# Spreading the sums of the output weights and the latent heads' parts over other heads of a hybrid attention block

## The chip, the cores and the metric

The kernel runs on one core of a Trainium2 chip. The metric is the device time of one execution in microseconds (us); three executions of the kernel before are given. Five engines work beside each other: TensorE (PE, the matmuls), VectorE (DVE), ScalarE (ACT), GpSimd (POOL, here mostly the issuer of small transfers) and SyncE (SP, the issuer of the weight loads).

## The reference, cut to what matters

```python
def hybrid_layer(x, cos, sin, pre_norm_w, w_in, ..., w_out, post_norm_w):     # x: 1 x 512 x 2048, float32
    h = rms_norm(x, pre_norm_w)
    sb_q, sb_k, sb_v, sb_gate, c_q, c_kv, k_rope, mla_gate = jnp.split(h @ w_in, split_pts, axis=-1)
    o_a = stick_breaking_attention(sb_q, sb_k, sb_v)          # 8 heads of 128, strictly causal
    ...
    o_b = chunk_causal_softmax_attention(q_mla, k_mla, v_mla)     # 8 heads from low-rank latents
    mixed = jnp.concatenate([o_a * jax.nn.silu(sb_gate), o_b * jax.nn.silu(mla_gate)], axis=-1)
    y = mixed @ w_out                                         # 512 x 2048 by 2048 x 2048
    return x + rms_norm(y, post_norm_w)
```

In stick-breaking attention the weight of key s for query t is beta[t,s] times the product of (1 - beta[t,j]) over the keys j between s and t, where beta is the sigmoid of the scaled score.

## The kernel before, in words

Everything is computed in float32 accuracy with split operands: a tile is cast to a high part (`whi`, `kh`, `vh`, `k1h`, ...; ScalarE) and the rest is taken as a low part (`wlo`, `kl`, `vl`, `k1l`, ...; VectorE), and a product is three matmuls, high by high, low by high and high by low (L123).

The latent (MLA) heads come first, then the eight stick-breaking heads, then the output product. Every projection of a stick-breaking head (the values `v` for four heads at a time, at heads 0 and 4; the queries `qp`, the keys `kp` and the gate `gps` for each head) comes out of one generator of steps, three matmuls each. `need(key)` draws steps until that product is complete; `fill(n)` draws n further steps between the steps of attention. The order of the matmuls is that of the program; much of the rest is ordered by the tile scheduler, except what `keep_in_program_order` pins.

The products `v`, `qp`, `kp` and `gps` share four PSUM banks. The values take all four; each is freed by a split of its own, `vh` on ScalarE and `vl` on VectorE (L103). So the queries that follow start when the first bank's `vl` is done, and the keys when the second's is.

The output product uses a scheme with sums of operand blocks in place of one block product. Two kinds of sums are prepared while the heads run:

- The weights' sums. The output weights are cut into 8 chunks; a chunk j has two halves u of four 128x512 tiles. `load_weight_parts(u, j)` loads four tiles (POOL's queue, L422, `wsum`), `weight_sums(u, j)` makes four subtractions (VectorE, L430) and stores each (POOL's queue, L431, `w_sums`). Both are pinned. The eight slots of the tag `qrt` hold one chunk: the next chunk's loads wait until the stores of the one before have read their tiles.
- The inputs' sums. After a stick-breaking head the mixed output is put aside (L754, L758) and its sums are made and stored (`head_sums`, L442 to L446: `s12`, `s4`). For a latent head `latent_parts` loads the mixed output (`mx`, tag `mv`, four slots), subtracts one half from the other (L458) and splits the result into `k1h` and `k1l`.

The order of this side work is written out by hand: `w_todo` says which chunks stand at which head, the first half of a chunk in front of the scores (after `fill(10)`), the second half behind the scores; the chunk for the next head is loaded at the end of a head. Heads 0 and 4 take two chunks: both have the second chunk's first half in front of the scores too, after a reload and `fill(30)`. The latent heads 0 to 3 are loaded and split behind the scores of head 6, the latent heads 4 to 7 at the start of head 7.

POOL issues all these loads and stores in the order of the program: an issue that waits holds up those behind it.

Of the kernel before, what the change touches and what calls it, by code (L numbers as in the profile page):

```python
# [24 lines left out]
H = 8  # L25
# [32 lines left out]
def block(ctx: ExitStack, tc: tile.TileContext, a: dict):  # L58
# [10 lines left out]
    def g(name, dt=F32, tag="g"):  # L69
        return gen.tile([P, S], dt, tag=tag, name=name, bufs=SLOTS[tag])  # L70
# [4 lines left out]
    def zbank(name, dt=F32):  # L75
        return psum.tile([P, S], dt, tag="z", name=name, bufs=2)
# [13 lines left out]
    def tokens(t, b):  # L90
        return t[:, b * P:(b + 1) * P]


    def split(hi, lo, src, scale=None, pin=False):
        if scale is None:
            i = act.copy(out=hi, in_=src)  # L96
            j = dve.tensor_tensor(out=lo, in0=src, in1=hi.bitcast(F32), op=ALU.subtract)  # L97
            if pin:
                tc.keep_in_program_order(i)
                tc.keep_in_program_order(j)  # L100
        else:
            act.activation(out=hi, in_=src, func=AF.Copy, scale=scale)
            dve.scalar_tensor_tensor(out=lo, in0=src, scalar=scale, in1=hi.bitcast(F32), op0=ALU.mult, op1=ALU.subtract)  # L103
# [24 lines left out]
    def mm3(out, sth, stl, mvh, mvl, first, last, **kw):  # L128
        mm(out, sth, mvh, first, False, **kw)
        mm(out, sth, mvl, False, False, **kw)  # L130
        mm(out, stl, mvh, False, last, **kw)
# [285 lines left out]
    def load_weight_parts(u, j):  # L417
        i, c = j // 2, slice((j % 2) * S, (j % 2 + 1) * S)
        w_parts[u, j] = []
        for gi, k in ((0, 0), (1, 0), (1, 4), (0, 4)):  # L420
            t = g("wsum", tag="qrt")
            tc.keep_in_program_order(pool.dma_start(out=t, in_=a["w_o"][2 * u + gi, k + i][:, c]))  # L422
            w_parts[u, j].append(t)

    def weight_sums(u, j):

        i, c = j // 2, slice((j % 2) * S, (j % 2 + 1) * S)
        b11, b12, b22, b21 = w_parts.pop((u, j))
        for n, (out, x, y) in ((0, (b11, b12, b11)), (2, (b12, b22, b12)), (1, (b22, b22, b11)), (3, (b21, b21, b22))):
            tc.keep_in_program_order(dve.tensor_tensor(out=out, in0=x, in1=y, op=ALU.subtract))  # L430
            tc.keep_in_program_order(pool.dma_start(out=w_sums[u][n][i][:, c], in_=out))  # L431

    def from_dram(src, w=S):
        t = g("mx", tag="mv")[:, :w]
        pool.dma_start(out=t, in_=src)
        return t

    def head_sums(h, x, y):

        t, s4 = g("st", tag="mv"), g("st4", tag="mv")[:, :HALF]  # L440
        s1, s2 = t[:, :HALF], t[:, HALF:]
        dve.tensor_tensor(out=s1, in0=x[:, HALF:], in1=y[:, HALF:], op=ALU.add)  # L442
        dve.tensor_tensor(out=s2, in0=s1, in1=x[:, :HALF], op=ALU.subtract)
        dve.tensor_tensor(out=s4, in0=y[:, :HALF], in1=s2, op=ALU.subtract)
        pool.dma_start(out=a_sums[h][0], in_=t)
        pool.dma_start(out=a_sums[h][1], in_=s4)  # L446

    k1, s12, k2, s4s = [], [], [], []

    def latent_parts(js, tag, steps=2):  # L450

        xs = []
        for j in js:
            x = from_dram(mixed[H + j])
            xs.append(x)
        for x in xs:
            fill(steps)
            tc.keep_in_program_order(dve.tensor_tensor(out=x[:, HALF:], in0=x[:, :HALF], in1=x[:, HALF:], op=ALU.subtract))  # L458
            hi, lo = g("k1h", F32R, tag), g("k1l", F32R, tag)
            split(hi, lo, x, pin=True)  # L460
            k1.append((hi, lo))
# [138 lines left out]
    def filler():  # L600
        yield from group_proj(a["w_ckv"], 320, kv_banks)
        done["ckv",] = True
        for h in range(H):
            done["mgate", h] = yield from gate(24 + h, "mg")
        for h in range(H):
            if h % 4 == 0:
                done["v", h // 4] = yield from sb_values(h // 4)
            done["q", h] = yield from sb_queries(h)
            done["k", h] = yield from sb_keys(h)
            done["gate", h] = yield from gate(h * 3 + 2, "gt")  # L610
        for u in range(2):
            yield from out_columns(u)

    steps = filler()
# [3 lines left out]
    def fill(n):  # L618
        for _ in range(n):
            next(steps, None)  # L620
        taken[0] += n

    def need(*key):
        while key not in done:
            fill(1)
        return done[key]
# [81 lines left out]
    for b in range(NB):  # L708
        x = ckvs[b][:, 256:320].rearrange("p (s f) -> p s f", s=2)
# [12 lines left out]
    def row_tiles(name):  # L722

        t0, t1, t2 = (g(name, tag="row") for _ in range(3))
        return [t0[:, 384:], t1[:, :256], t0[:, :384], t2]
# [31 lines left out]
    def put_aside(i, t):  # L757
        pool.dma_start(out=mixed[i], in_=t)  # L758
# [58 lines left out]
    mixed = [dram.tile([P, S], F32, name=f"mixed{i}") for i in range(2 * H)]  # L817
# [66 lines left out]
    def load_parts(j):  # L884
        for u in range(2):
            load_weight_parts(u, j)

    w_todo = {0: [0, 1], 1: [2], 2: [3], 3: [4], 4: [5, 6], 5: [7]}
    load_parts(0)
    for h in range(H):  # L890
        late = None
        for n, j in enumerate(w_todo.get(h, ())):
            if n:
                weight_sums(1, late)
                load_parts(j)
                fill(30)
            else:
                fill(10)
            weight_sums(0, j)
            late = j  # L900
        if h == H - 1:
            latent_parts(range(4, 8), "g")
        kh, kl = need("k", h)
        qh, ql = need("q", h)
        fill(6 if h < H - 1 else 4)
        rows = row_tiles("beta")
        x = from_dram(mixed[H + h])
        for b in range(NB):
            n = (b + 1) * P
            w = max(n, 256)  # L910
            z = zbank("z")
            mm3(z[:, :w], tokens(qh, b), tokens(ql, b), kh[:, :w], kl[:, :w], True, True)
            dve.tensor_tensor(out=z[:, n - P:n], in0=z[:, n - P:n], in1=m_sb, op=ALU.add)
            keep, prod, beta = g("keep", tag="tr"), g("prod", tag="tr"), rows[b]
            act.activation(out=keep[:, :n], in_=z[:, :n], func=AF.Sigmoid, scale=rq_neg[:, b:b + 1])
            act.activation(out=beta, in_=z[:, :n], func=AF.Sigmoid, scale=rq_pos[:, b:b + 1])
            dve.tensor_tensor_scan(out=prod[:, :n][:, ::-1], data0=keep[:, :n][:, ::-1], data1=zero.broadcast_to([P, n]),
                                   initial=1.0, op0=ALU.mult, op1=ALU.add)
            dve.tensor_tensor(out=beta[:, :n - 1], in0=beta[:, :n - 1], in1=prod[:, 1:n], op=ALU.mult)
            fill((1, 3, 3, 7)[b])  # L920
        if late is not None:
            weight_sums(1, late)
        if h == H - 2:
            latent_parts(range(4), "qrt", 0)
        cur = Weighted(rows, need("v", h // 4), (h % 4) * P)
        for j in range(NB):
            cur.turn(j)
            fill(3)
            cur.add(j)
        for j in w_todo.get(h + 1, ())[:1]:  # L930
            load_parts(j)
        out = cur.finish(need("gate", h))
        put_aside(h, out)
        head_sums(h, x, out)
# [58 lines left out]
```

## Time and profile before

| what | value |
|---|---|
| three runs | 853.22, 857.14 and 1027.36 us (median 857.14) |
| the profiled execution | 856.84 us, of which the traced span is 855.1 us |
| granted TensorE clock, mean | 0.991 |
| PE busy | 827.4 us (97%), 4002 matmul records |
| DVE / ACT / POOL busy | 524.2 / 371.0 / 134.1 us (61%, 43%, 16%) |

Busy time is the time in which the trace has an instruction running on an engine; 855.1 less 827.4 us is what TensorE idles, its start and the end of the kernel included. An idle stretch is put down to what ended last before it. A queue's transfer is timed from its issue to its landing.

### The profile page before, as it was taken

What the parts mean: (1) busy time and instruction counts of PE and PEld (TensorE: products, weight loads), DVE (VectorE), ACT (ScalarE), POOL (GpSimd) and SP (SyncE); (2) the same over time, 40 slices, a digit from 0 to 9 for tenths busy, and PEclk for the clock granted to TensorE, in tenths of its full rate; (3) what the DMA queues carried; (4) which work ended last, traced back from release to release, by engine and by line L of the source; (5) the groups of instructions that cost most, each with busy time, mean ns of one, the idle gap of its engine ahead of it and who ended that gap; (6) DMA issues with size and microseconds to landing.
All of it is one profiled execution on the core that took longest, in us unless ns stands there. A gap on an engine that the chain in (4) does not pass through costs nothing.

```text
span 855.1 us, 11124 instructions
## 1 busy us (share of the span) xinstructions
PE 827.4 (97%) x4002; PEld 692.5 (81%) x4002; DVE 524.2 (61%) x914; ACT 371.0 (43%) x626; POOL 134.1 (16%) x270
## 2 busy tenths in 40 slices
PE   8999999999999997999999999999999899999995
PEld 5889988888888885888888888888888787788874
DVE  5566765565665544366666754376566676965667
ACT  7742655545555322243333322242433564655531
POOL 1000000000000043014233152014020223000002
PEclk9999999999999998999999999999999999999998
DMA  9923322222221168248476568338352657766965
GB/s 327 344 80 105 99 80 81 80 93 80 81 92 63 63 227 289 89 142 305 151 260 196 198 235 344 98 126 295 115 181 94 216 183 257 269 213 218 329 225 196
DMA packets 49607, 152.27 MB, mean 178 GB/s; under 512 B 7297, under 2 KB 7569, under 8 KB 49553
## 3 DMA queue, kind: packets, MB, share of 16 engines
q1 hardware_dynamic: 31680, 94.91, 32.7%
q0 software_dynamic: 16576, 54.56, 18.1%
q10 hardware_dynamic: 1296, 2.11, 0.6%
q8 instruction: 31, 0.51, 0.2%
q14 instruction: 24, 0.19, 0.1%
HBM read 123.24 MB, written 28.31 MB: 177 GB/s over the span
## 4 chain that ended last, share of the span: by engine, by line
PE 48%; DVE 5%; DMA 3%; issue 3%; ACT 1%; POOL 1%; DVEq 0%; POOLq 0%; ACTq 0%
PE qp L123 10%; PE kp L123 9%; PE gps L123 8%; PE v L123 5%; PE sx L123 4%; PE sv L123 4%; PE sz L123 3%; PE av L123 2%; PE z L123 2%; PE sy L123 1%; DVE xr L597 1%; DMA mx<-mixed 1%; PE tp L126 1%; DMA raw<-in_w_o 1%; DVE wlo L97 1%
## 5 line engine op out<-in xcount | busy, mean ns | idle before, releaser
L96 ACT CAST whi<-raw 128x1024 fp32r<-128x1024 f32 (+2 forms) x149 | 153.2, 1028 | 249.3 <-issue 55.3
L97 DVE TENSOR_TENSOR wlo<-raw,whi 128x1024 fp32r<-128x1024 f32 (+2 forms) x149 | 177.7, 1194 | 108.0 <-ACT whi L96 107.5
L123 PE MATMUL gps<-hh,whi 128*128 128x512 f32 x256 | 102.0, 398 | 0.0
L123 PE MATMUL gps<-hl,whi 128*128 128x512 f32 x256 | 100.1, 391 | 0.0
L123 PE MATMUL gps<-hh,wlo 128*128 128x512 f32 x256 | 100.0, 390 | 0.0
L123 PE MATMUL qp<-hh,whi 128*128 128x512 f32 x128 | 52.8, 412 | 6.0 <-DVE vl L103 6.0
L430 DVE TENSOR_TENSOR wsum<-wsum 128x512 f32<-128x512 f32 x64 | 44.1, 689 | 23.1 <-DMA wsum<-in_w_o 22.1
L123 PEld LDWEIGHTS gps<-hh,wlo 128*128 128x128 f32 x256 | 48.0, 188 | 10.6
L96 ACT CAST th<-tp 128x512 fp32r<-128x512 f32 (+1 forms) x64 | 27.2, 425 | 63.6 <-PE tp L126 63.4
L97 DVE TENSOR_TENSOR tl<-tp,th 128x512 fp32r<-128x512 f32 (+1 forms) x64 | 31.1, 487 | 38.2 <-ACT th L96 37.7
L123 PEld LDWEIGHTS gps<-hl,whi 128*128 128x128 f32 x256 | 48.3, 189 | 7.6
L123 PEld LDWEIGHTS gps<-hh,whi 128*128 128x128 f32 x256 | 48.2, 188 | 7.6
L123 PE MATMUL v<-whi,hh 128*128 128x512 f32 x128 | 51.0, 398 | 0.4 <-DVE gt L345 0.4
L123 PE MATMUL qp<-hh,wlo 128*128 128x512 f32 x128 | 50.6, 395 | 0.0
L123 PE MATMUL qp<-hl,whi 128*128 128x512 f32 x128 | 50.4, 394 | 0.0
L123 PE MATMUL v<-whi,hl 128*128 128x512 f32 x128 | 49.9, 390 | 0.0
L123 PE MATMUL v<-wlo,hh 128*128 128x512 f32 x128 | 49.9, 390 | 0.0
L123 PE MATMUL kp<-hh,whi 128*128 128x512 f32 x128 | 49.9, 390 | 0.0
L123 PE MATMUL kp<-hl,whi 128*128 128x512 f32 x128 | 49.9, 390 | 0.0
L123 PE MATMUL kp<-hh,wlo 128*128 128x512 f32 x128 | 49.8, 389 | 0.0
L431 POOL DMA_DIRECT2D w_sums<-wsum x64 | 34.4, 540 | 97.7 <-DVE wsum L430 92.7
L422 POOL DMA_DIRECT2D wsum<-in_w_o x64 | 34.7, 548 | 10.0 <-DMA w_sums<-wsum 7.8
(301 smaller groups left out, 1869.7 us busy)
## 6 DMA issues: line engine op xcount, KB each, us to landing
raw<-in_w_t SPq DMA_DIRECT2D x64, 512.0 KB, 3.4
wsum<-in_w_o POOLq DMA_DIRECT2D x64, 256.0 KB, 5.3
w_sums<-wsum POOLq DMA_DIRECT2D x64, 256.0 KB, 5.2
raw<-w_sums SPq DMA_DIRECT2D x32, 512.0 KB, 4.0
raw<-in_w_o SPq DMA_DIRECT2D x20, 512.0 KB, 4.4
raw<-in_w_v SPq DMA_DIRECT2D x16, 512.0 KB, 3.3
mx<-mixed POOLq DMA_DIRECT2D x24, 256.0 KB, 4.2
xs<-in_x SPq DMA_DIRECT2D x16, 256.0 KB, 6.4
```

What stands on the lines that cost most here:

```text
L96: i = act.copy(out=hi, in_=src)
L97: j = dve.tensor_tensor(out=lo, in0=src, in1=hi.bitcast(F32), op=ALU.subtract)
L123: tc.keep_in_program_order(pe.matmul(out=out, lhsT=lhsT, rhs=rhs, start=start, stop=stop, **kw))
L126: tc.keep_in_program_order(pe.transpose(out, in_, identity))
L422: tc.keep_in_program_order(pool.dma_start(out=t, in_=a["w_o"][2 * u + gi, k + i][:, c]))
L430: tc.keep_in_program_order(dve.tensor_tensor(out=out, in0=x, in1=y, op=ALU.subtract))
L431: tc.keep_in_program_order(pool.dma_start(out=w_sums[u][n][i][:, c], in_=out))
L597: dve.scalar_tensor_tensor(out=o, in0=y, scalar=r2, in1=o, op0=ALU.mult, op1=ALU.add)
```

## The change

The number of chunks, the loads, the subtractions, the stores and the splits stays as it was; so does the order of the matmuls. What moves:

- The first head takes one chunk (0), behind `fill(24)` in place of `fill(10)`; the heads 1, 2 and 3 take the chunks 1, 2 and 3 (2, 3 and 4 before).
- Head 4, where the second four heads' values are made, has: the first half of chunk 4; its second half, now ahead of the scores; the load of chunk 5; `fill(36)`; both halves of chunk 5, with `fill(4)` between; the load of chunk 6; the first half of chunk 6 behind the scores and its second half behind the products with the values. Head 5 keeps chunk 7.
- The latent heads' parts are made two at a time, at the start of the heads 1, 2, 6 and 7; their `mx` are loaded at the end of the head before, ahead of that head's put-aside. At the heads 6 and 7 their splits lie in `qrt`, at 1 and 2 in `g`.

```diff
-    def latent_parts(js, tag, steps=2):
-
-        xs = []
+    latent_xs = []
+
+    def load_latents(js):
+        latent_xs.extend(from_dram(mixed[H + j]) for j in js)
+
+    def latent_parts(js, tag):
+
         for j in js:
-            x = from_dram(mixed[H + j])
-            xs.append(x)
-        for x in xs:
-            fill(steps)
+            fill(2)
+            x = latent_xs.pop(0)
             tc.keep_in_program_order(dve.tensor_tensor(out=x[:, HALF:], in0=x[:, :HALF], in1=x[:, HALF:], op=ALU.subtract))
...
-    w_todo = {0: [0, 1], 1: [2], 2: [3], 3: [4], 4: [5, 6], 5: [7]}
+    first_chunk = {0: 0, 1: 1, 2: 2, 3: 3, 4: 4, 5: 7}
+    latents = {1: (0, 1), 2: (2, 3), 6: (4, 5), 7: (6, 7)}
     load_parts(0)
     for h in range(H):
-        late = None
-        for n, j in enumerate(w_todo.get(h, ())):
-            if n:
-                weight_sums(1, late)
-                load_parts(j)
-                fill(30)
-            else:
-                fill(10)
-            weight_sums(0, j)
-            late = j
-        if h == H - 1:
-            latent_parts(range(4, 8), "g")
+        behind = []
+        if h in first_chunk:
+            fill(10 if h else 24)
+            weight_sums(0, first_chunk[h])
+            behind = [(1, first_chunk[h])]
+        if h == H // 2:
+
+            weight_sums(1, 4)
+            load_parts(5)
+            fill(36)
+            weight_sums(0, 5)
+            fill(4)
+            weight_sums(1, 5)
+            load_parts(6)
+            behind = [(0, 6), (1, 6)]
+        if h in latents:
+            latent_parts(latents[h], "g" if h < 6 else "qrt")
...
-        if late is not None:
-            weight_sums(1, late)
-        if h == H - 2:
-            latent_parts(range(4), "qrt", 0)
+        if behind:
+            weight_sums(*behind.pop(0))
         cur = Weighted(rows, need("v", h // 4), (h % 4) * P)
         for j in range(NB):
             cur.turn(j)
             fill(3)
             cur.add(j)
-        for j in w_todo.get(h + 1, ())[:1]:
-            load_parts(j)
+        if behind:
+            weight_sums(*behind.pop(0))
+        if h + 1 in first_chunk:
+            load_parts(first_chunk[h + 1])
+        if h + 1 in latents:
+            load_latents(latents[h + 1])
```

What VectorE has in a row up to the splits of the first values, before (`mix` is the last latent head's output, `wsum` are the weights' sums, `wlo` low parts of projection weights, `vl` the low parts of the values, bank by bank):

```order
L754 TENSOR_TENSOR mix<-av,mg 128x512
L97 TENSOR_TENSOR wlo<-raw,whi 128x1024
L430 TENSOR_TENSOR wsum<-wsum 128x512 x5
L97 TENSOR_TENSOR wlo<-raw,whi 128x1024
L430 TENSOR_TENSOR wsum<-wsum 128x512 x3
L97 TENSOR_TENSOR wlo<-raw,whi 128x1024
L430 TENSOR_TENSOR wsum<-wsum 128x512 x3
L97 TENSOR_TENSOR wlo<-raw,whi 128x1024
L430 TENSOR_TENSOR wsum<-wsum 128x512
L103 SCALAR_TENSOR_TENSOR vl_0_3409<-v_0_2927,rstd,vh_0_3408 128x512
```

The same place on VectorE after the change:

```order
L756 TENSOR_TENSOR mix<-av,mg 128x512
L97 TENSOR_TENSOR wlo<-raw,whi 128x1024
L430 TENSOR_TENSOR wsum<-wsum 128x512 x4
L97 TENSOR_TENSOR wlo<-raw,whi 128x1024 x3
L103 SCALAR_TENSOR_TENSOR vl_0_3385<-v_0_2927,rstd,vh_0_3384 128x512
```

Of the twelve subtractions in front of the first bank's split four are left, those of chunk 0's first half; the four of chunk 1, which was loaded here after chunk 0, stand at another head now.

What VectorE has in a row up to the splits of the second four heads' values (head 4), before; the last four `wsum` here are the first half of chunk 6:

```order
L430 TENSOR_TENSOR wsum<-wsum 128x512
L97 TENSOR_TENSOR wlo<-raw,whi 128x1024
L430 TENSOR_TENSOR wsum<-wsum 128x512
L97 TENSOR_TENSOR wlo<-raw,whi 128x1024 x2
L430 TENSOR_TENSOR wsum<-wsum 128x512 x4
L97 TENSOR_TENSOR wlo<-raw,whi 128x1024 x2
L103 SCALAR_TENSOR_TENSOR vl_0_5045<-v_0_4681,rstd,vh_0_5044 128x512
```

The same place on VectorE after the change; the last eight `wsum` are the two halves of chunk 5:

```order
L430 TENSOR_TENSOR wsum<-wsum 128x512
L97 TENSOR_TENSOR wlo<-raw,whi 128x1024
L430 TENSOR_TENSOR wsum<-wsum 128x512
L97 TENSOR_TENSOR wlo<-raw,whi 128x1024 x2
L430 TENSOR_TENSOR wsum<-wsum 128x512 x4
L97 TENSOR_TENSOR wlo<-raw,whi 128x1024
L430 TENSOR_TENSOR wsum<-wsum 128x512 x4
L97 TENSOR_TENSOR wlo<-raw,whi 128x1024
L103 SCALAR_TENSOR_TENSOR vl_0_5041<-v_0_4677,rstd,vh_0_5040 128x512
```

Four subtractions more stand in front of the second values' splits, one `wlo` ahead of them. Later in head 4 VectorE's row was the gate's `gt` (L348), then the first low part of the transposed weights `tl` (128x512), then `wlo`; now two subtractions of chunk 6 stand between `gt` and `tl` and two behind it.

What ScalarE has in a row from the last weights' cast of head 6's end to the first scores of head 7 (`kr` are the scaled keys, `mx` behind `kh` a loaded sum `s12` of head 0), before:

```order
L96 CAST qh<-qp 128x512
L96 CAST whi<-raw 128x1024
L96 CAST k1h<-mx 128x512 x2
L96 CAST whi<-raw 128x1024
L96 CAST k1h<-mx 128x512
L96 CAST kh<-kr 128x512
L96 CAST k1h<-mx 128x512
L96 CAST kh<-mx 128x512
L915 ACTIVATE keep<-z,rq_neg 128x128
```

The same place on ScalarE after the change:

```order
L96 CAST qh<-qp 128x512
L96 CAST k1h<-mx 128x512
L96 CAST whi<-raw 128x1024
L96 CAST k1h<-mx 128x512
L96 CAST whi<-raw 128x1024
L96 CAST kh<-mx 128x512
L96 CAST kh<-kr 128x512
L923 ACTIVATE keep<-z,rq_neg 128x128
```

Two of the four latent casts are gone from here, and the cast of the loaded sum, which was behind that of the head's keys, is in front of it.

## Rows read from the trace of the kernel before

**Rows 1.** The page: busy us, share of the span and instructions of each engine.

```profile
PE 827.4 (97%) x4002; PEld 692.5 (81%) x4002; DVE 524.2 (61%) x914; ACT 371.0 (43%) x626; POOL 134.1 (16%) x270
```

**Rows 2.** Waits of PE: us in total, times, longest.

```profile
PE qp L123 <- DVE vl L103: 6.0, 1, 6.0
PE sz L123 <- DVE wlo L97: 2.8, 3, 1.3
PE z L123 <- ACT kh L96: 1.5, 1, 1.5
PE z L123 <- DVE kl L97: 1.3, 1, 1.3
```

**Rows 3.** Timeline, first values, PE: start, us, instruction [idle before <- releaser].

```profile
329.24 0.39 PE L123 MATMUL v<-whi,hl 128*128 128x512 f32 x1
335.66 0.79 PE L123 MATMUL qp<-hh,whi 128*128 128x512 f32 x1 [6.03 <-DVE vl L103]
```

**Rows 4.** The chain of waits from 300 to 360 us: start, length, what.

```profile
335.66 12.55 PE qp L123 x48
348.21 10.88 PE kp L123 x48
```

**Rows 5.** Windows: busy time per engine, granted clock, DMA share, GB/s.

```profile
336.00:341.00 5.00, 5.00 (x17) 3.98 (x17) 2.71 (x4) 0.00 (x0) 0.00 (x0) 0.74 0.86 270
500.00:520.00 20.00, 20.00 (x91) 16.62 (x90) 11.32 (x16) 4.22 (x4) 11.08 (x22) 1.00 0.88 323
```

**Rows 6.** Timeline, first values, DVE, then ACT.

```profile
331.06 2.14 DVE L430 TENSOR_TENSOR wsum<-wsum 128x512 f32<-128x512 f32 x3 [9.01 <-DMA wsum<-in_w_o]
334.86 2.06 DVE L103 SCALAR_TENSOR_TENSOR vl<-v,rstd,vh 128x512 fp32r<-128x512 f32 x3
327.62 2.05 ACT L102 ACTIVATE vh<-v,rstd 128x512 fp32r<-128x512 f32 x3 [2.35 <-PE v L123]
```

**Rows 7.** Head 4, second values: DVE's timeline, POOL's last load, PE's chain.

```profile
522.08 2.87 DVE L430 TENSOR_TENSOR wsum<-wsum 128x512 f32<-128x512 f32 x4 [2.66 <-DMA wsum<-in_w_o]
529.07 1.23 DVE L97 TENSOR_TENSOR wlo<-raw,whi 128x1024 fp32r<-128x1024 f32 x1 [2.98 <-ACT whi L96]
532.10 2.11 DVE L103 SCALAR_TENSOR_TENSOR vl<-v,rstd,vh 128x512 fp32r<-128x512 f32 x3 [1.81 <-ACT vh L102]
521.22 0.55 POOL L422 DMA_DIRECT2D wsum<-in_w_o  x1 [0.92 <-DMA w_sums<-wsum]
533.38 10.88 PE qp L123 x48
```

**Rows 8.** The tile wsum from 500 to 560 us: transfers of both directions.

```profile
DMA to landing us min/median/max: 2.6/6.7/9.8
```

**Rows 9.** Head 4, turn to the values: DVE's timeline, then PE's.

```profile
572.60 0.68 DVE L97 TENSOR_TENSOR tl<-tp,th 128x512 fp32r<-128x512 f32 x1
573.97 0.39 PE L123 MATMUL av<-tl,vh 128*128 128x512 f32 x1
```

**Rows 10.** Head 7: timeline of DVE, ACT, POOL and PE.

```profile
670.67 0.43 DVE L458 TENSOR_TENSOR mx<-mx 128x256 f32<-128x256 f32 x1 [2.48 <-DMA mx<-mixed]
668.74 1.04 ACT L96 CAST whi<-raw 128x1024 fp32r<-128x1024 f32 x1
672.66 0.62 ACT L96 CAST kh<-kr 128x512 fp32r<-128x512 f32 x1
664.77 1.08 POOL L435 DMA_DIRECT2D mx<-mixed x2 [0.86 <-DMA s<-st]
668.09 0.39 PE L123 MATMUL kp<-hh,wlo 128*128 128x512 f32 x1
671.49 0.39 PE L123 MATMUL gps<-hh,wlo 128*128 128x512 f32 x1
```

**Rows 11.** The tile mx from 655 to 680 us: transfers of both directions.

```profile
DMA to landing us min/median/max: 2.8/3.6/5.3
```

**Rows 12.** Head 1, before its keys' scaling: DVE's timeline.

```profile
397.67 0.69 DVE L372 TENSOR_TENSOR kr<-kp,rstd_bc 128x512 f32<-128x512 f32 x1 [3.31 <-PE kp L123]
```

## The prediction, made before the changed kernel had run

> **What bounds the kernel now.** I began with the page: TensorE has a matmul running for 97% of the span [rows 1], and the order of its matmuls stays as it is, so the change can only take away or add idle time between them. Next I read the waits of TensorE [rows 2]. The reader is to see one long wait, 6.0 us for a low part of the values, two shorter ones of 1.5 and 1.3 us in front of a head's scores, and the waits for output weights (`sz`), which lie behind the heads and are not touched. Then I read the timeline at the long wait [rows 3]: the last values' matmul starts at 329.24, the first queries' at 335.66. Last came the chain and the windows [rows 4, 5]: the 48 matmuls of the queries behind that gap take 12.55 us, the 48 of the keys 10.88 us, and the granted clock of the 5 us behind the gap is 0.74 on average, so a part of them ran at the lower of its two levels (1.2 GHz), after TensorE had stood still. The long wait costs 6.03 us and 12.55 − 10.88 = 1.67 us more.
>
> All that the change could take away is therefore 6.03 + 1.67 + 1.46 + 1.30 = 10.46 us, some 1.2% (1.5 and 1.3 us in [rows 2] are the two waits of head 7, one each).
>
> **First values: 7.70 us go.** VectorE stood idle for 9.01 us until a load for the weights' sums landed, then had three subtractions (2.14 us), a `wlo` and a fourth subtraction before the first `vl` at 334.86 [rows 6]. ScalarE had made the `vh` from 327.62 on [rows 6]: values were waiting for a VectorE that was held by another job's load. These subtractions are of chunk 1, which the first head reloads into the slots of chunk 0, and the order shows them gone from here. What is left in front are four of chunk 0, whose loads were issued long before and which also stood there before, and `wlo`s. So `vl` can follow its `vh`: 327.62 + 0.68 = 328.3, and `vl` done at about 329.0 (0.68 for each is the pitch of three in 2.05 us, [rows 6]). The queries could start one pitch of matmuls after 329.24, at about 329.5. The second bank is needed 10.88 us later, and is no limit. Nothing is late next: 6.03 us go, and without the gap no reason is left for the lower clock: 1.67 us go with it. The bound from below is zero, if the gap stays.
>
> **Second values: nothing, with some 2 us of cover.** Head 4 now has four subtractions more in front of the same kind of split, and the transfers for one chunk more (eight loads and eight stores). Before, VectorE's idle time there was 2.66 us in front of four subtractions, 2.98 us in front of a `wlo`, and 1.81 us for `vh` [rows 7]. The four new ones cost 2.87 us [rows 7] and stand between the `wlo` behind 522.08 + 2.87 and that at 529.07: they fill the 2.98 us and lean a little on the 1.81. `vl` at 532.10 follows `vh`, and the queries start at 533.38 [rows 7] without a wait in [rows 2], so 532.10 + 0.68 = 532.8 leaves another 0.6 us. What decides is whether the loads are there. The last load of the reload is issued at 521.22 [rows 7]; transfers of this tile landed after 2.6 to 9.8 us, 6.7 in the middle [rows 8]: at 523.8 to 531.0. At 531.0 the last subtraction, the `wlo` and the `vl` end at 531.0 + 0.7 + 1.2 + 0.7 = 533.6, that is 0.2 us late; at 6.7 there is no wait. The reload stands behind the same halves of a chunk as before and the `fill` is 36 in place of 30, so the loads come earlier against the matmuls, not later. I take 0, and keep 0.2 as its bound.
>
> Here the transfers run against a busy system: from 500 to 520 us the DMA engines are busy for 0.88 of the time, at 323 GB/s [rows 5], and the median landing is 6.7 us [rows 8]. The Trainium skill (DMA: Bandwidth & Descriptors, Anatomy of one DMA — SWDGE (gpsimd) path) fits one such transfer by 2.0 us plus its bytes over 436,000 per us, an estimate of 2.6 us for 256 KB; the smallest of [rows 8] agrees, the median doesn't. By that figure the second values could not wait at all, and the rival below would fall away. The same page (Issuing engines are not separate DMA queues) says that transfers of all issuers share the same engines and interleave, which speaks for the median, and against moving more of them into head 4; no run so far shows which of the two holds when a chunk more is moved there.
>
> **Head 4's turn to the values: plus 0.69 us.** Two subtractions of chunk 6 now stand between `gt` and the first `tl`. `tl` began at 572.60 right behind `gt` and took 0.68; its matmul started at 573.97 [rows 9]. With two subtractions at 2.87 / 4 = 0.72 us apart [rows 7] in between, `tl` ends at 572.60 + 1.43 + 0.68 = 574.71, or, at the 0.68 of a single one, 574.64; the matmul before has no wait, so it is late by 0.67 to 0.74; I take 0.69. The bounds are 0 (if `gt` comes earlier than before) and 1.4 (if the two behind it hold the second `tl` too). The loads of chunk 6 are issued ahead of the scores, as soon as chunk 5's stores have read their tiles, and are taken to have landed.
>
> **Head 7's scores: minus 2.76 us.** Before, VectorE waited 2.48 us for the third latent head's load, so its subtraction came at 670.67, and behind it, in its row, the scaling of the keys; their cast `kh` came at 672.66 although the keys' matmuls had started their last at 668.09 and the gate's at 671.49 [rows 10]. The scores thus waited 1.46 and 1.30 us [rows 2]. Now two latent heads stand here in place of four, and they are loaded before head 6's put-aside, not in head 7. The scaling can follow the keys at about 668.5, its cast (0.62, [rows 10]) and its low part (0.68, as `tl`'s, [rows 9]) would end by 670. On ScalarE, however, the cast of a loaded sum stands in front of `kh` now. Its load is issued behind the store of head 6's sums, no earlier than 664.27 to 664.77, where the loads stood before [rows 10]. Loads of `mx` land after 2.8 to 5.3 us, 3.6 in the middle [rows 11]: 668.4 in the middle, 670.1 at most. ScalarE's `whi` ends at 668.74 + 1.04 = 669.8 [rows 10]; the loaded sum's cast ends at 670.4 (670.7), `kh` at 671.0 (671.3), `kl` at 671.7 (672.0); the scores need them at about 671.7 and 671.95. So no wait, or 0.1 us: the saving is 2.76, with a bound of 0 if that load is late.
>
> **Heads 1, 2 and 6 get two latent heads each.** On VectorE that is 2 × (0.43 + 0.68) = 2.2 us [rows 9, 10] in front of the keys' scaling, which at head 1 stood idle for 3.31 us until TensorE gave the keys [rows 12]. Cost 0. Their loads wait for nothing of this head. All else (the chunks 1 to 3 a head later each, `fill(24)`) lies at places where no wait is in [rows 2]: 0.
>
> **Sum.** −6.03 − 1.67 + 0.69 − 2.76 = −9.77 us. The profiled execution took 856.84 us, so 847.1; it lies 0.30 below the median of the runs, 857.14, so the forecast is 847.4.
>
> **Rivals.**
>
> A, head 7 still waits. The cast of the loaded sum holds `kh`, if its load lands 2 us or more later than the middle. For it: the load is issued while other stores run. Against: [rows 11]. The 2.76 us stay: 850.1.
>
> B, the stall moves to the second values. The second half of chunk 5 waits for its loads there as chunk 1's first half did at the first. For it: the share of 0.88 [rows 5]. Against: 2 us of cover, and 9.8 us as the longest landing [rows 8]. If all 7.70 us come back there, 847.4 + 7.7 = 855.1.
>
> C, slower than before. The latent heads' loads at 1, 2 and 6 land late and hold VectorE in front of the keys' scaling as they did at head 7: 2.76 us at each of the three, with nothing won at head 7. Then 3 × 2.76 + 0.69 − 7.70 = +1.3, 858.4. It begins to cost where a load comes later than the 3.31 − 2.2 = 1.1 us that are left [rows 12]; it ends on the slower side only if it happens at all three. Against: the loads are issued a head's end earlier.
>
> D, the first gap stays, because something else than chunk 1 held `vl`: 847.4 + 7.7 = 855.1 too. Against: [rows 6] name the load, and the order shows the subtractions gone.
>
> **How the numbers follow.** The forecast has 0.71, A 0.14, B 0.08, C 0.04, D 0.03. The range takes in the forecast and A, 0.85 together. Its low end is the forecast for the lowest run shown, 853.22 − 9.77 = 843.5; the high end is 852.0, A with 1.9 us, half of the spread between the two lower runs, above. A measurement of this kernel tells about 2% (17 us) from no change. The most that can go is 10.46 us, and C is 1.3 us slower: faster by that 0.03, slower 0.02, within it 0.95.
>
> **What would show it.** In the changed kernel's waits of TensorE the row of the queries waiting for `vl` is gone, and the queries' 48 matmuls of the first head take 10.9 us. The rows of scores waiting for `kh` and `kl` at head 7 are gone. A wait of `av` for `tl` of about 0.7 us is new. The mean clock rises a little above 0.991, and TensorE's idle time falls from 27.7 us to about 20 (the 1.67 us were busy time). The prediction is wrong if a wait for `vl` shows at the second values, if scores wait at the heads 1, 2, 6 or 7, or if weights (`whi`, `wlo`) come late in head 4.

## The result, and the profile after

The changed kernel takes 844.58 us (median of 4 runs, 842.05 to 845.96) where the kernel before takes 857.77 in the same comparison: a ratio of 0.986 with an interval of 0.981 to 0.991. The 857.77 takes in one slow run of 1027.36 us, which the ratio leaves out; without it the kernel before has a median of 857.14, and the difference is 12.6 us in place of 13.2. The forecast was 847.4, in a range of 843.5 to 852.0. The profiled execution of the changed kernel took 845.96 us, 10.88 less than the 856.84 of the one before; its span is 844.3 us.

The page of the changed kernel, busy us, share of the span and instructions of each engine:

```profile
PE 825.5 (98%) x4002; PEld 691.4 (82%) x4002; DVE 524.9 (62%) x914; ACT 371.1 (44%) x626; POOL 134.1 (16%) x270
```

The waits of TensorE in the changed kernel that bear on the forecast (us in total, times, longest):

```profile
PE sz L123 <- DVE wlo L97: 2.7, 3, 1.3
PE av L123 <- DVE tl L97: 0.7, 2, 0.5
PE z L123 <- ACT beta L924: 0.5, 1, 0.5
```

Beside [rows 2], the wait for `vl` and the two waits of the scores are gone, and a wait of `av` for `tl` is new. The wait of `z` for `beta`, 0.5 us at the first head, was there before too. Busy time fell by 1.9 us, though the same matmuls ran. The first values, in the chain of waits from 300 to 360 us (start, length, what):

```profile
329.45 10.88 PE qp L123 x48
340.33 10.88 PE kp L123 x48
```

The timelines of TensorE and VectorE there:

```profile
329.29 0.39 PE L123 MATMUL qp<-hh,whi 128*128 128x512 f32 x1
...
328.17 2.11 DVE L103 SCALAR_TENSOR_TENSOR vl<-v,rstd,vh 128x512 fp32r<-128x512 f32 x3 [1.81 <-ACT vh L102]
```

The queries start one pitch behind the last values' matmul (the pitch is the time from one start to the next where nothing waits, 0.23 us here), `vl` waits for `vh` alone, and the 48 matmuls of the queries take as long as those of the keys, 10.88 us where [rows 4] had 12.55.

The second values at head 4, VectorE's timeline, and the sixth and the last of POOL's eight loads of the reload:

```profile
514.72 0.69 DVE L430 TENSOR_TENSOR wsum<-wsum 128x512 f32<-128x512 f32 x1 [3.18 <-DMA wsum<-in_w_o]
515.84 2.15 DVE L430 TENSOR_TENSOR wsum<-wsum 128x512 f32<-128x512 f32 x3 [0.43 <-DMA wsum<-in_w_o]
517.90 1.22 DVE L97 TENSOR_TENSOR wlo<-raw,whi 128x1024 fp32r<-128x1024 f32 x1
520.15 2.87 DVE L430 TENSOR_TENSOR wsum<-wsum 128x512 f32<-128x512 f32 x4 [1.03 <-DMA wsum<-in_w_o]
522.94 1.22 DVE L97 TENSOR_TENSOR wlo<-raw,whi 128x1024 fp32r<-128x1024 f32 x1
524.23 2.11 DVE L103 SCALAR_TENSOR_TENSOR vl<-v,rstd,vh 128x512 fp32r<-128x512 f32 x3
...
511.15 0.55 POOL L422 DMA_DIRECT2D wsum<-in_w_o  x1 [1.78 <-DMA w_sums<-wsum]
...
513.05 0.55 POOL L422 DMA_DIRECT2D wsum<-in_w_o  x1 [0.19 <-issue]
```

The chain of waits there:

```profile
525.51 10.88 PE qp L123 x48
```

The transfers of the tile `wsum` from 490 to 555 us:

```profile
DMA to landing us min/median/max: 2.6/6.5/10.4
```

A window ahead of the second values (busy time by engine, granted clock, DMA share, GB/s):

```profile
495.00:520.00 25.00, 25.00 (x112) 20.71 (x111) 13.56 (x19) 4.22 (x4) 12.95 (x24) 1.00 0.96 333
```

TensorE doesn't wait here. But VectorE waits three times for loads (3.18, 0.43 and 1.03 us), runs without a pause to `vl`, and the first `vl` ends at 524.23 + 0.68 = 524.9, only 0.6 us ahead of the queries at 525.51.

Head 4's turn to the values, VectorE, then TensorE:

```profile
564.72 1.41 DVE L430 TENSOR_TENSOR wsum<-wsum 128x512 f32<-128x512 f32 x2
566.05 0.69 DVE L97 TENSOR_TENSOR tl<-tp,th 128x512 fp32r<-128x512 f32 x1
...
565.87 0.39 PE L123 MATMUL av<-th,vh 128*128 128x512 f32 x1
566.79 0.50 PE L123 MATMUL av<-tl,vh 128*128 128x512 f32 x1 [0.53 <-DVE tl L97]
```

Head 7, VectorE, ScalarE and TensorE:

```profile
661.45 0.69 DVE L372 TENSOR_TENSOR kr<-kp,rstd_bc 128x512 f32<-128x512 f32 x1 [2.71 <-PE kp L123]
...
662.23 0.61 ACT L96 CAST kh<-mx 128x512 fp32r<-128x512 f32 x1
662.75 0.62 ACT L96 CAST kh<-kr 128x512 fp32r<-128x512 f32 x1
...
664.42 0.39 PE L123 MATMUL gps<-hh,wlo 128*128 128x512 f32 x1
664.65 0.28 PE L123 MATMUL z<-kh,qh 128*128 128x256 f32 x1
664.76 0.28 PE L123 MATMUL z<-kl,qh 128*128 128x256 f32 x1
```

The scaling now waits for TensorE's keys and for nothing else (before it stood behind a latent subtraction that waited 2.48 us for its load, [rows 10]), the loaded sum was there when ScalarE came to it, and the scores follow the gate's matmuls without a gap.

**Where the time came from, by starts.** The order of the matmuls is the same, so the start of each can be compared in the two traces; the lead is by how much the changed kernel is ahead. It is 0.18 us at the last of the first values, grows by 6.19 us at the first queries (329.24 to 335.66 is 6.42, less the pitch of 0.23) and by 1.51 over the 48 queries (from the first query to the first keys 335.66 to 348.05, 12.39 us, before, and 329.29 to 340.17, 10.88 us, after). It falls by 0.70 at head 4's turn (565.87 to 566.79 is 0.92, less the 0.22 of before) and by 0.11 at the matmul behind it. At the two gaps of head 7 it grows by 1.62 and 1.57, and by 0.11 behind them. Small steps are left: −0.31 at head 7's first `tl`, +0.61 at the first `sz` of the output product, +0.2 behind it. At the last matmul it is 845.18 − 834.29 = 10.89 us, the whole of the profiled difference.

The chain gives the queries 12.55 − 10.88 = 1.67 us where the starts give 1.51. It counts a piece from its first start where that matmul waited, and from the modelled end of the matmul before, 0.16 us later than the start, where it didn't. So 1.67 goes with the idle time of 6.03, and 1.51 with the 6.19: both make 7.70.

### The profile page after: what moved, and what is told of

Read it like the earlier page. It is cut to its first block, busy times and chain, and to the rows that moved or that the text cites. A ratio compares the mean times of both kernels' runs of the same rounds, so it can differ in the third digit from the quotient of the medians.

```text
span 844.3 us, 11111 instructions
## 1 busy us (share of the span) xinstructions
PE 825.5 (98%) x4002; PEld 691.4 (82%) x4002; DVE 524.9 (62%) x914; ACT 371.1 (44%) x626; POOL 134.1 (16%) x270
## 4 chain that ended last, share of the span: by engine, by line
PE 83%; DVE 7%; issue 4%; DMA 3%; ACT 2%; POOL 1%; SPq 0%; DVEq 0%; POOLq 0%; ACTq 0%
PE gps L123 17%; PE kp L123 10%; PE v L123 10%; PE qp L123 10%; PE cq L123 5%; PE sv L123 4%; PE av L123 4%; PE sx L123 3%; PE sz L123 3%; PE mz L123 3%; PE mqp L123 3%; PE ckv L123 2%; PE tp L126 2%; PE qrp L123 1%; PE mv L123 1%
```

## Experiments

**1. The chunks alone.** The latent heads' parts are those of before:

```diff
...
-        if h in latents:
-            latent_parts(latents[h], "g" if h < 6 else "qrt")
+        if h == H - 1:
+            latent_parts(range(4, 8), "g")
...
+        if h == H - 2:
+            latent_parts(range(4), "qrt", 0)
...
-        if h + 1 in latents:
-            load_latents(latents[h + 1])
```

> The chunks of the weights' sums stand as after the change, the latent heads' parts as before it. Theory (the gain is a sum of separate places on VectorE's row): the queries' wait for vl (6.0 us) and the lower clock behind it (1.67 us) are gone, a wait of av for tl of 0.5 us is new, the scores' waits for kh and kl at head 7 (1.46 and 1.30 us) stay; about 7.2 us less than before, 850.5 us. Rival (the two parts of the change act on each other: the latent heads' loads and splits at the heads 6 and 7 lost time only because the chunks stood late): the waits at head 7 go too, and the time is that of the changed kernel, 844.6.

850.03 us, ratio 0.991 (0.988 to 0.994). Three of the waits of TensorE in this kernel:

```profile
PE z L123 <- ACT kh L96: 1.8, 1, 1.8
PE z L123 <- DVE kl L97: 1.3, 1, 1.3
PE av L123 <- DVE tl L97: 0.5, 1, 0.5
```

The wait for `vl` is gone, the waits at head 7 stay. By starts, too, 7.7 us are gained at the first values and 0.81 lost at head 4's turn, as in the changed kernel. The parts don't depend on each other there; the rival fell.

**2. The latent heads alone.** The chunks are those of before (`w_todo`), the latent heads' parts those of the change.

```diff
...
-        if h == H - 1:
-            latent_parts(range(4, 8), "g")
+        if h in latents:
+            latent_parts(latents[h], "g" if h < 6 else "qrt")
...
-        if h == H - 2:
-            latent_parts(range(4), "qrt", 0)
...
+        if h + 1 in latents:
+            load_latents(latents[h + 1])
```

> The latent heads' parts are made two at a time at the heads 1, 2, 6 and 7, the chunks stand as before the change. Theory: the wait for vl of 6.0 us and the slower queries behind it stay, the scores' waits at head 7 are gone; 3.2 us less than before, 854.5. Rival: at the heads 1 and 2, where the chunks 2 and 3 are summed too, the latent splits hold the keys' splits, and new waits of z for kh or kl of 0.5 to 2.8 us at each take the gain back: 855 to 860.

852.66 us, ratio 0.994 (0.992 to 0.997), some 2 us better than expected. The long wait of TensorE:

```profile
PE qp L123 <- DVE vl L103: 6.9, 1, 6.9
```

The chain of waits at the first queries:

```profile
334.83 13.98 PE qp L123 x48
```

The long wait stays (6.9 us, and 13.98 us for 48 matmuls in place of 12.55), no wait of the scores for `kh` or `kl` is left at any head, and the new places at heads 1 and 2 cost nothing. The forecast's rival C would have shown here, at the same places as in the changed kernel, and doesn't. The two parts' median gains, 7.8 and 5.2 us, make 13.05; the whole has 12.6 to 13.2. What made this median 2 us better than expected is not shown: by starts head 7 gives 3.30 us here, as in the changed kernel, and another 1.65 us of the profiled difference lie at the kernel's start, which this edit doesn't touch (see the last part of "Why the prediction was right").

**3. The transfers in the first head, without the subtractions that wait for them.** The changed kernel with this edit:

```diff
-            fill(10 if h else 24)
+            fill(10)
             weight_sums(0, first_chunk[h])
             behind = [(1, first_chunk[h])]
+        if h == 0:
+            weight_sums(*behind.pop())
+            load_parts(1)
+            fill(30)
...
-        if h + 1 in first_chunk:
+        if h > 0 and h + 1 in first_chunk:
```

> The changed kernel, but in the first head chunk 0's second half is summed ahead of the scores and chunk 1 is reloaded where it was before the change (fill 10, then fill 30); its sums still stand at head 1. So the eight loads run against the first values, but no subtraction that waits for them stands on VectorE's row in front of vl. Theory (the row): no wait for vl, the time of the changed kernel, 844.6, within 1 us. Rival (the transfers: sixteen DMA engines are busy at 0.93 there, and whatever stands there is late): a wait for vl, whi or wlo of some 2 to 6 us at the first values, 847 to 852.

842.44 us, ratio 0.982 (0.979 to 0.986). The windows around the first values:

```profile
316.00:326.00 10.00, 10.00 (x45) 8.27 (x45) 5.89 (x7) 2.35 (x3) 5.59 (x11) 1.00 0.94 314
326.00:336.00 10.00, 10.00 (x46) 8.27 (x45) 5.23 (x6) 4.49 (x6) 0.89 (x2) 1.00 0.82 294
```

The DMA engines are nearly as busy as before the change (0.94 and 0.82, where these stretches had 1.01 and 0.93), far busier than in the changed kernel (0.74 and 0.32), and TensorE is busy without a gap at full clock. The transfers by themselves were not the cost; four subtractions in VectorE's row that waited for them were. Another wait is gone as well: the scores of the first head waited once, 0.49 us, for `beta`, while chunk 0's second half stood in VectorE's row there; it is summed ahead of the scores now, and by starts 0.77 us are gained there.

**4. One number in the kernel before.**

```diff
-                fill(30)
+                fill(30 if h else 40)
```

> The kernel before, with one number changed: chunk 1's first half in the first head stands after fill(40) in place of fill(30), which puts its four subtractions behind the splits of the values and not in front of them. All of chunk 1 stays in the first head. Theory (the place in the row, not the amount of work in the first head): the wait for vl and the lower clock behind it go, 7.9 us less than before, 849.9; the waits at head 7 stay. Rival (the amount: two chunks don't fit into the first head): the wait moves to the keys' splits or to the first turn of head 0, and 3 us or more of the 7.9 come back, 853 or more.

850.51 us (846.15 to 851.61), ratio 0.991 (0.988 to 0.995). VectorE's timeline:

```profile
327.23 2.11 DVE L103 SCALAR_TENSOR_TENSOR vl<-v,rstd,vh 128x512 fp32r<-128x512 f32 x3 [1.81 <-ACT vh L102]
...
331.43 2.86 DVE L430 TENSOR_TENSOR wsum<-wsum 128x512 f32<-128x512 f32 x4
```

Both chunks are still in the first head, the DMA engines are as busy as before (0.95 and 1.00 in the two stretches of experiment 3), and the gap is gone: the subtractions stand behind the splits, where their tiles have landed. So the place did it. That chunk 1 left the first head is one way to that.

**5. Head 4's turn.** The changed kernel, with the second half of chunk 6 directly behind the last turn:

```diff
             cur.turn(j)
+            if behind and j == NB - 1:
+                weight_sums(*behind.pop(0))
             fill(3)
             cur.add(j)
-        if behind:
-            weight_sums(*behind.pop(0))
```

> The changed kernel, but head 4's second half of chunk 6 is written directly behind the last turn of the weights, which puts its four subtractions behind all tl on VectorE's row (two stood in front of the first tl, two in front of the second). Theory (these two subtractions cost 0.69 us at head 4's turn): the wait of av for tl of 0.53 us there is gone, and TensorE is 0.6 to 0.7 us earlier behind it. Rival: the later stores of this half hold the reload of chunk 7, whose sums then come late at head 5, and a wait of 0.5 us or more shows there in its place.

844.21 us, the time of the changed kernel. `tl` is no longer waited for at head 4 (TensorE gained 0.80 us there by starts), but the rival's wait came: `PE z <- DVE kl`, 0.69 us of idle time, 1.07 by starts, at head 5. VectorE's timeline there:

```profile
582.81 0.69 DVE L430 TENSOR_TENSOR wsum<-wsum 128x512 f32<-128x512 f32 x1 [2.49 <-DMA wsum<-in_w_o]
584.84 2.14 DVE L430 TENSOR_TENSOR wsum<-wsum 128x512 f32<-128x512 f32 x3 [1.33 <-DMA wsum<-in_w_o]
586.90 0.68 DVE L372 TENSOR_TENSOR kr<-kp,rstd_bc 128x512 f32<-128x512 f32 x1
```

Chunk 7 is loaded into the slots of chunk 6, whose stores are later now; its subtractions wait 2.49 and 1.33 us and stand in front of the keys' scaling.

**6. Two latent heads, loaded late.** The changed kernel, but head 7's two latent heads are loaded at its start:

```diff
+        if h == H - 1:
+            load_latents(latents[h])
         if h in latents:
             latent_parts(latents[h], "g" if h < 6 else "qrt")
...
-        if h + 1 in latents:
+        if h + 1 in latents and h + 1 < H - 1:
```

> The changed kernel, but the loads of the last two latent heads stand at the start of head 7 and not at the end of head 6: two latent heads in place of four, loaded as late as before the change. Theory A (two loads less are enough, the place of the loads adds nothing): no wait of the scores at head 7, the time of the changed kernel. Theory B (it is the early load): VectorE waits for mx again in front of the keys' scaling, and scores wait 1 to 3 us for kh and kl.

845.96 us (844.19 to 848.16). TensorE waits 1.5 us for `kh` and 0.3 us for `kl`. ScalarE's timeline:

```profile
662.45 1.05 ACT L96 CAST whi<-raw 128x1024 fp32r<-128x1024 f32 x1
665.63 0.62 ACT L96 CAST kh<-mx 128x512 fp32r<-128x512 f32 x1 [2.14 <-DMA mx<-s]
666.16 0.61 ACT L96 CAST kh<-kr 128x512 fp32r<-128x512 f32 x1
```

Theory B is nearer: the place of the loads counts. The last link is the forecast's rival A: the loaded sum's load lands late, its cast stands in front of that of the keys, and the scores wait for it. By starts 2.4 us are lost there against the changed kernel, so of the 3.3 us of head 7 the early loads give 2.4, and two latent heads less at most the rest.

**7. The second values' cover.** The changed kernel, with the last of chunk 5's eight tiles loaded twice:

```diff
             tc.keep_in_program_order(pool.dma_start(out=t, in_=a["w_o"][2 * u + gi, k + i][:, c]))
+            if (u, j) == (1, 5) and (gi, k) == (0, 4):
+                tc.keep_in_program_order(pool.dma_start(out=t, in_=a["w_o"][2 * u + gi, k + i][:, c]))
             w_parts[u, j].append(t)
```

> The changed kernel, but the last of chunk 5's eight tiles is loaded twice into its slot, the second time when the first has landed, so that the sums in front of the second values' vl get their last tile some 3 to 6 us later. Theory (the second values have little cover, 0.6 us by the trace of the changed kernel, where vl ended 0.6 us before the queries began): queries wait for vl there, 1 to 5 us, and if the clock falls behind the gap some 1 to 2 us more; 846 to 851. Rival (some 2 us of cover and a scheduler's row with room, as forecast): a wait under 1 us, 844 to 846.

846.40 us (844.96 to 847.91). TensorE's wait:

```profile
PE qp L123 <- DVE vl L103: 2.8, 1, 2.8
```

VectorE's timeline in this kernel:

```profile
524.03 0.69 DVE L432 TENSOR_TENSOR wsum<-wsum 128x512 f32<-128x512 f32 x1 [3.83 <-DMA wsum<-in_w_o]
525.78 2.06 DVE L103 SCALAR_TENSOR_TENSOR vl<-v,rstd,vh 128x512 fp32r<-128x512 f32 x3
```

The chain of waits behind it:

```profile
526.58 12.75 PE qp L123 x48
```

VectorE waited 3.83 us for the tile, TensorE 2.75 us for `vl`, and the 48 queries took 12.75 us: the wait of the first values comes back at the second, at 2.75 + 1.87 us. Of 3.83 us only 1.1 were covered. The times are closer than these 4.6 us: in the profiled runs the changed kernel loses 1.6 us at its start and 2.4 in the output product against this one, both far from this edit.

**8. Both edits together.** Experiment 3 with the edit of experiment 5.

> The two edits together that were each ahead of the changed kernel: chunk 1 reloaded in the first head (chunk 0's second half summed ahead of the scores), and chunk 6's second half behind the last turn. Theory: the gains of 0.7 us each at separate places add up, 841.7 where the first alone had 842.4. Rival: with both, the time is that of the first alone, since what is gained at head 4 is waited for later.

842.37 us, ratio 0.983 (0.979 to 0.986): that of experiment 3 alone. The wait for `tl` is gone, a wait of 0.6 us for `kl` stands at head 5, as in experiment 5; by starts 0.79 us are gained at head 4 and 1.2 lost at head 5 against experiment 3. The rival holds.

**9. Two and two.** Experiment 3, with chunk 6's second half behind the second and the third turn:

```diff
-    def weight_sums(u, j):
+    def weight_sums(u, j, first=0, last=4):
...
             cur.turn(j)
+            if behind and 0 < j < NB - 1:
+                weight_sums(*behind[0], 2 * j - 2, 2 * j)
...
-        if behind:
-            weight_sums(*behind.pop(0))
...
```

> The version with chunk 1 reloaded in the first head, and chunk 6's second half at head 4 in two pairs: two subtractions behind the second turn of the weights, two behind the third, where VectorE stands idle for 1.4 and 2.1 us. Theory: no wait of av for tl at head 4 beyond 0.2 us, and no new wait of scores at head 5, since the stores come early enough for chunk 7; 0.7 us less than the version with the reload alone, 841.7 beside 842.4. Rival: the pairs hold the following tl, and a wait of av of 0.5 us shows there; 842.4.

841.55 us (840.25 to 841.57), ratio 0.981 (0.979 to 0.984): the best of all, beside 844.59 (843.52 to 845.46) of the changed kernel on the same chip. The runs of the two don't overlap; the intervals of their ratios, 0.9786 to 0.984 and 0.9829 to 0.9878, just do. VectorE's timeline:

```profile
566.81 1.41 DVE L430 TENSOR_TENSOR wsum<-wsum 128x512 f32<-128x512 f32 x2
568.57 0.42 DVE L97 TENSOR_TENSOR tl<-tp,th 128x256 fp32r<-128x256 f32 x1 [0.35 <-ACT th L96]
568.91 1.41 DVE L430 TENSOR_TENSOR wsum<-wsum 128x512 f32<-128x512 f32 x2
571.07 0.29 DVE L97 TENSOR_TENSOR tl<-tp,th 128x128 fp32r<-128x128 f32 x1 [0.75 <-ACT th L96]
```

Each pair lies in VectorE's idle time in front of a `tl`; both `tl` still wait for ScalarE, and chunk 7 comes in time. By starts, against the changed kernel on the same chip, 0.77 us are gained at the first head and 0.80 at head 4; the other half of the 3.0 us between the medians is not explained by the edits.

**10. The changed kernel and experiment 3 again,** beside experiment 9 on one chip.

> The changed kernel, beside the two others on the same chip. Theory: 844.6 as at first, with waits of sz for wlo in the output product of 1.3 to 2.7 us in all. If these waits go by the run and not by the kernel, they may be 1.3 us here; if by the kernel, 2.7.

> The version with chunk 1 reloaded in the first head, again. Theory: some 2 us less than the changed kernel, of which 0.7 us are the wait of the second scores for beta at the first head (gone here, since chunk 0's second half isn't summed behind these scores) and the rest the waits of sz for wlo, which were 1.3 us here and 2.7 there. Rival: these two us are differences between runs, and both kernels take the same time within 0.5 us.

844.59 us (843.52 to 845.46), ratio 0.985 (0.983 to 0.988), and 842.82 us (841.63 to 844.58), ratio 0.983 (0.981 to 0.986). The waits of `sz` for `wlo` in the changed kernel, again:

```profile
PE sz L123 <- DVE wlo L97: 1.3, 1, 1.3
```

The same waits with the reload, again:

```profile
PE sz L123 <- DVE wlo L97: 1.8, 2, 1.3
```

The same changed kernel had 2.7 us of them at first and 1.3 us here: they go by the run. Between the medians of the two kernels are 1.8 us; their intervals overlap, so that the reload is faster is likely and not shown. By starts 0.76 us are its own (the wait for `beta`).

## Why the prediction was right

**The first values** carry the gain as forecast: −7.70 against 6.19 + 1.51 = 7.70 us by starts. That it was VectorE's row is shown by experiments 3 and 4, which keep the transfers, or all the work, in the first head, and the gap is gone; that it needed no help from the other part by experiment 1. Rival D is out.

**Head 7** was under-sized: −2.76 against 3.30 us. The mechanism was as forecast (experiments 1, 2 and 6). The step took the idle time of [rows 2], which counts from the modelled end of the matmul before, 0.39 us after its start; a matmul that doesn't wait would follow after a pitch of 0.23 or 0.11. At each of the gaps, the first values' too, 0.16 to 0.27 us more are lost than the idle time says, and behind the last one another 0.11.

**The second values** cost nothing, as forecast, but "some 2 us of cover" was wrong, and that the term came out at 0 is partly luck. The cover was to be the 1.81 us that VectorE waited for `vh`, and 0.6 us behind `vl`; the loads held VectorE three times, the 1.81 us are gone from `vl`'s row, and the 0.6 us are what was left. Two readings failed. The loads were to come earlier against the matmuls, but the last is issued 525.51 − 513.05 = 12.5 us ahead of the queries, where it was 533.38 − 521.22 = 12.2 before. And the step counted one subtraction behind the last landing. In the trace four stand behind an earlier one: the first subtraction of chunk 5's second half, which takes that half's first two tiles, starts at 520.15, 9.0 us after the second of them was issued at 511.15, and 520.15 + 2.87 + 1.22 = 524.24 is where `vl` starts. Where the last tile alone is late the bound of the step is good: it puts the queries 0.2 us late at a landing of 9.8 us, so 2.7 at 12.3; in experiment 7 the tile was there 524.0 − 511.7 = 12.3 us after its first issue at 511.70, and TensorE waited 2.75 us. Rival B was nearer than its 0.08 said. From 495 to 520 us the DMA share is 0.96, and the tile's transfers landed after 2.6 to 10.4 us, 6.5 in the middle. The Trainium skill (DMA: Bandwidth & Descriptors, Anatomy of one DMA — SWDGE (gpsimd) path) gives one transfer a fixed cost and one by its size, an estimate of 2.6 us here; this trace agrees only for the fastest. The same page of the Trainium skill (Issuing engines are not separate DMA queues) says that the transfers of all issuers run on the same 16 engines and interleave. The slower landings fit that, but no run here shows that it is their cause.

**Head 4's turn** cost 0.70 us at the matmul that the forecast names (+0.69, worked out from starts, where the idle time has 0.53), and 0.11 at the next one. It is avoidable (experiment 9).

**The heads 1, 2 and 6** cost nothing; rival C did not show in the changed kernel or in experiment 2. **Rival A** did not happen in the changed kernel, but is real (experiment 6).

**What the sum lacked.** For the profiled execution the forecast was 847.1 and the result 845.96: −9.77 against −10.89 us by starts. The steps of 0.54 us at head 7, −0.11 at head 4, +0.18 ahead of the first values, −0.31 at head 7's `tl` (its matmuls come earlier, and a split of a loaded sum stands in front of it, as before), +0.61 at the first `sz` and 0.2 behind it make these 1.1 us. So more went than the 10.46 us that the prediction took for the most: it counted idle time, and it took the output product's waits as they were.

The other part of the distance to 844.58 is between runs: the profiled execution of the changed kernel was the slowest of its four. The traces show one source. The first 20 us (busy time by engine, granted clock, DMA share, GB/s) in the changed kernel of experiment 10, then in the kernel of experiment 9:

```profile
0.00:20.00 20.00, 16.98 (x56) 11.00 (x57) 10.30 (x16) 13.75 (x23) 3.98 (x15) 0.91 0.90 330
0.00:20.00 20.00, 16.78 (x61) 10.97 (x62) 10.08 (x16) 13.37 (x23) 3.97 (x15) 1.00 0.92 327
```

No edit touches this stretch. In four traces (the kernel before, the changed kernel, experiment 6 and the changed kernel again) its mean clock is 0.91, so a part of it ran at the lower of TensorE's two levels (1.2 GHz); in the other nine it is 1.00. The wait of TensorE's transposes `tpc` for `cq`, 0.61 us long in every trace, ends at 63.3 to 63.7 us in the four and at 61.7 to 62.6 us in the nine. So some 1 to 2 us come and go at the start with the run; the comparison of the two main traces is free of it, since both have it. Why the clock falls there in some runs, and what moves the waits for the output product's first weights, was not tried.

## What to carry to other kernels

A side job of an in-order engine that waits for its own load holds what stands behind it, however idle the engine is on average (61% busy here): move its place in the row until its load has landed, and look at the next waiting place, since slots that come free later load the next chunk later. A lost stretch is better read as the difference of two starts less the pitch than as the idle time of the row, and the two ways are not to be mixed in one sum. Where the scheduler orders the row, a pin to the instruction written before it doesn't fix a place: the half written behind the products of head 4 ran in front of the first `tl`, until it was written behind a turn.

## What the runs showed of the hardware that had not been expected

How much the clock takes back behind a gap doesn't follow the length of the gap. Behind waits of 6.03, 6.85 and 2.75 us (the kernel before, experiments 2 and 7) the 48 matmuls of the queries took 12.39, 13.82 and 12.58 us, from the first start to the start behind them, in place of 10.88, so 1.51, 2.94 and 1.70 us were lost. One reason stands in the windows inside the gap, first in the kernel before, then in experiment 7 (the columns as above):

```profile
332.00:335.60 3.60, 0.00 (x0) 0.00 (x0) 3.57 (x6) 0.00 (x0) 1.97 (x4) 0.50 0.82 299
523.50:526.50 3.00, 0.33 (x2) 0.00 (x0) 2.47 (x4) 2.00 (x3) 2.35 (x5) 1.00 1.00 396
```

In the long gap the granted clock was down (0.50) while TensorE had nothing to run, so a part of the low stretch cost nothing. In the short one it was still 1.00, and fell when the queries had begun (0.57 from 526.5 to 530.5 us): all of the low stretch fell on matmuls. The gap of experiment 2 was at 0.50 too (331 to 334.8 us) and still lost the most, since its clock stayed low longer (0.52 from 334.8 to 341 us); why it did is not shown.

At head 7 two waits in a row of 1.46 and 1.30 us in the kernel before left the granted clock at 1.00, as did waits of 1.61 and 1.31 us in experiment 4. In experiment 1 waits of 1.84 and 1.30 us were followed by a clock of 0.76 and by matmuls 0.43 us apart in place of 0.23. The kernel before, then experiment 1:

```profile
672.00:678.00 6.00, 3.36 (x16) 2.75 (x17) 5.66 (x12) 3.98 (x9) 2.18 (x4) 1.00 0.62 189
665.00:672.00 7.00, 4.74 (x16) 3.85 (x17) 5.80 (x12) 3.52 (x9) 1.80 (x4) 0.76 0.71 222
```

A wait of that size can thus cost another 1.5 us or nothing. The five runs of experiment 4 may show the same: 846.15 and 847.15 us at a mean clock of 0.995 and 0.996, and 850.51 to 851.61 us at 0.991 to 0.992. Where the clock fell in the latter three is not shown, since the trace is of the run of 847.15 us.
